# A two-layer hybrid block on one core: half-column inverse levels, and attention scores of both partition halves in turn

## Chip, cores, metric

The kernel runs on one core of one Trainium2 chip. The metric is the device time of one execution in microseconds (us). Everything below is float32 data; products of the large projections are done in two or three passes on a rounded part and a remainder (fp32r), the small ones inside the mixer in plain float32.

## What is computed

The reference is a stack of two layers over 256 positions of width 1024. Each layer is a half-weighted SwiGLU block, a mixer of three branches with gates, and a second SwiGLU block:

```python
for l in range(DEPTH):                                    # DEPTH = 2
    x = x + 0.5 * swiglu(rms_norm(x, ffa_norm[l]), ffa_w_in[l], ffa_w_out[l])
    h = rms_norm(x, mix_norm[l])
    (c_q, c_kv, k_rope, g_q, g_k, g_v, g_b, g_a, g_z, m_qkv, gate_logits) = split_cols(h @ w_in[l], IN_SPLITS)
    o_mla = mla_branch(...)                               # causal attention, 8 heads, 96 wide
    o_gdn = gdn_branch(...)                               # gated delta rule, 4 heads, 128 wide
    o_moba = moba_branch(...)                             # block attention, 8 heads, 64 wide
    up = jnp.einsum('bsnw,nwd->bsnd', branches, w_branch[l])
    x = x + jnp.sum(sigmoid(gates) * up, axis=2) @ w_out[l]
    x = x + 0.5 * swiglu(rms_norm(x, ffb_norm[l]), ffb_w_in[l], ffb_w_out[l])
```

With 256 positions the block attention has a single block, so it is causal attention with 64-wide heads. The delta rule needs the inverse of a unit lower triangular matrix for each half of 128 positions and each head; the reference solves with it, the kernel builds the inverse from 16x16 diagonal blocks and doubles the block size level by level.

## The kernel before

A phase (SwiGLU block or mixer) is a list of steps. A step loads one 512 KB tile of weights, splits it in two (a rounded part by ScalarE, line 260, a remainder by VectorE, line 261) and multiplies it on TensorE (lines 280 to 282, 309 and 311, 340 to 342, 965 and 966). `phase` walks the steps; between half steps it calls `tick`, which lets every spawned generator emit its next piece. A `yield n` in a generator waits for n ticks. So small work (attention, delta rule, epilogues) is laid between half steps of 12 large matmuls (lines 340 to 342; 8 for lines 965 and 966), and each engine runs what it was given in about the order in which it was emitted.

Names that matter here:

- `acc` and `pm` (lines 113 to 125) hand out PSUM banks from one pool of `BANKS` = 6; at most three are accumulators in the mixer, and `hold` lets at most `BANKS` - 4 = 2 score tiles be held at once. `done` gives the hold back once the exponentials that read the tile have been emitted.
- `attention` (line 560) serves the causal attention (heads 96 wide) and the block attention. Its `plan` has entries "s0" (scores of the first 128 queries, four heads, 128 keys each), "s1" (scores of the second 128 queries, two heads, 256 keys each) and "o" (two heads' product with the values); between entries it waits `Y_ATT` = 3 ticks. `scores` issues one matmul for each head (line 574), adds the mask with one bf16 matmul against an identity (line 576), takes the row maximum on VectorE (lines 581 and 582), one tick later the exponentials on ScalarE (line 586, each followed by a read of its accumulated sum), and a tick after that the reciprocal (line 590) and the scaling by it (line 592). `outputs` waits until the four tiles of its two heads exist, transposes the probabilities on TensorE (lines 604 to 606), copies them out of PSUM (line 608), and multiplies them with the values (lines 613 and 614): the first head writes partitions 0 to 63 of one bank, the second 64 to 127.
- In the block attention (plan at line 1078) even heads lie on partitions 0 to 63 of the transposed queries and keys, odd heads on 64 to 127. Each score tile holds heads of one half: "s0" with (0, 2, 4, 6), then (1, 3, 5, 7); "s1" with (0, 2), (1, 3), (4, 6), (5, 7).
- `invert` (line 731) is the inverse, for both halves c = 0, 1 of the positions. After `small` has brought the 16x16 blocks it runs two levels (loop at line 769): four matmuls, one for each head, of the coupling blocks with the inverse so far (line 772), a ScalarE copy (line 774), a GpSimd product for the next level (line 776), four matmuls with the transposed inverse (line 780), and a VectorE sum (line 783) that keeps only the even blocks' columns: of 128 columns, blocks of 16 (then 32) columns at even places, 64 in all. `back` (line 665) then transposes the result (line 669) and copies it (line 670). A third level on 64x64 quarters follows (lines 789 to 796).
- A float32 matmul shows as two weight loads and two matmul records in the trace. Records of four heads therefore count eight.

Of the kernel before, what the change touches and what calls it, by code (L numbers as in the profile page):

```python
# [11 lines left out]
AF = mybir.ActivationFunctionType  # L12
OP = mybir.AluOpType
AX = mybir.AxisListType
# [23 lines left out]
BANKS = 8 - NTP  # L38
# [43 lines left out]
class Kern:  # L82
# [32 lines left out]
        self.held["acc"] += 1  # L115
        return self.ps.tile([128, 512], F32, name=self.nm("acc"), tag="bank", bufs=BANKS)

    def hold(self):

        while self.held["pm"] >= BANKS - 4:  # L120
            yield 1
        self.held["pm"] += 1

    def done(self, what):
        self.held[what] -= 1
# [434 lines left out]
    def attention(self, plan, getq, getk, getv, rq, oT):  # L560
# [3 lines left out]
        nc = self.nc  # L564
# [1 line left out]
        P0, P1 = {}, {}  # L566
        left = [len(plan)]

        def scores(hs, n, w, q0, dst):
            t = q0 // 128  # L570
            yield from self.hold()
            ps = self.pm().rearrange("p (h k) -> p h k", h=n)
            for i, h in enumerate(hs):
                mm(ps[:, i, :], getq(h)[:, q0:q0 + 128], getk(h)[:, 0:w], start=(i == 0), stop=False,  # L574
                   skip_group_check=True)
            mm(ps[:, :, w - 128:w], self.identb, self.maskA[:, None, :].to_broadcast([128, n, 128]), start=False, stop=True,
               skip_group_check=True)
            dh = hs[1] - hs[0]
            rqs = rq[t][:, hs[0]:hs[-1] + 1:dh]
            mx, nb, sm, rs = (self.sm(4)[:, 0:n] for _ in range(4))  # L580
            nc.vector.tensor_reduce(mx, ps, axis=AX.X, op=OP.max)
            nc.vector.scalar_tensor_tensor(nb, mx, -1.0, rqs, op0=OP.mult, op1=OP.mult)
            yield 1
            P = self.b2().rearrange("p (h k) -> p h k", h=n)
            for h in range(n):
                nc.scalar.activation(P[:, h, :], ps[:, h, :], AF.Exp, scale=rqs[:, h:h + 1], bias=nb[:, h:h + 1],
                                     accum_out=sm[:, h:h + 1])
            self.done("pm")
            yield 1
            nc.vector.reciprocal(rs, sm)  # L590
            for h in range(n):
                nc.scalar.activation(P[:, h, :], P[:, h, :], AF.Copy, scale=rs[:, h:h + 1])
            for i, h in enumerate(hs):
                dst[h] = P[:, i, :]
            left[0] -= 1

        def outputs(hs):
            while not all(h in P0 and h in P1 for h in hs):
                yield 1
            yield 1  # L600
            PT = []
            for h in hs:
                pt = self.tp().rearrange("p (j k) -> p j k", j=4)
                nc.tensor.transpose(pt[:, 0, :], P0[h], self.ident)
                nc.tensor.transpose(pt[:, 1, :], P1[h][:, 0:128], self.ident)
                nc.tensor.transpose(pt[:, 2, :], P1[h][:, 128:256], self.ident)
                PT.append(self.b2())
                nc.scalar.copy(PT[-1][:, 0:384], pt[:, 0:3, :].rearrange("p j k -> p (j k)"))
            yield 1
            o = self.pm()[:, 0:256]  # L610
            for i, h in enumerate(hs):
                ov = o[64 * i:64 * i + 64, :]
                mm(ov, getv(0, h), PT[i][:, 0:256], start=True, stop=False, skip_group_check=True)  # L613
                mm(ov[:, 128:256], getv(1, h), PT[i][:, 256:384], start=False, stop=True, skip_group_check=True)
            k = hs[0] // 2
            self.split(oT[k // 2][:, k % 2, 0, :], oT[k // 2][:, k % 2, 1, :], o)
            left[0] -= 1

        for what, hs in plan:
            if what == "o":  # L620
                yield from outputs(hs)
            else:
                self.spawn(scores(hs, 4, 128, 0, P0) if what == "s0" else scores(hs, 2, 256, 128, P1))
            yield Y_ATT
# [3 lines left out]
    def gdn(self, ready, sil, beta, g, zs, oT):  # L628


        nc = self.nc
# [107 lines left out]
        def invert(c):  # L739
# [27 lines left out]
            back(zz[:, :, 0, :], zz[:, :, 1, :])  # L767
            yield 1
            for l in range(LEVELS - 1):
                p = v4(self.pm())  # L770
                for h in range(H):
                    mm(p[:, h, :], cm[:, h, :], zz[:, h, 0, :], start=True, stop=True)
                t1 = v4(self.b2())
                nc.scalar.copy(t1, p)
                cm = v4(self.b2())
                nc.gpsimd.tensor_tensor(cm, nk, brow(self.lev[l + 1]), op=OP.mult)
                yield Y_INV
                p = v4(self.pm())
                for h in range(H):
                    mm(p[:, h, :], zz[:, h, 1, :], t1[:, h, :], start=True, stop=True)  # L780
                even = lambda z: z.rearrange("p h (m s b) -> p h m s b", s=2, b=16 << l)[:, :, :, 0, :]
                v = even(zz[:, :, 0, :])
                nc.vector.tensor_tensor(v, even(p), v, op=OP.add)
                yield Y_INV
                back(zz[:, :, 0, :], zz[:, :, 1, :])

# [95 lines left out]
    def mixer(self, l, norm_after):  # L882
# [177 lines left out]
        def attend():  # L1060
# [11 lines left out]
            while not all(("turned", ("mT", i), 1) in d for i in range(2)) or ("mv", 1) not in d:  # L1072
# [2 lines left out]
            d["oT", 2] = [newT() for _ in range(2)]  # L1075
            sl = lambda z, h: z[64 * (h % 2):64 * (h % 2) + 64, h // 2, :]
            yield from self.attention(
                [("s0", (0, 2, 4, 6)), ("s0", (1, 3, 5, 7)), ("s1", (0, 2)), ("s1", (1, 3)), ("o", (0, 1)),
                 ("s1", (4, 6)), ("o", (2, 3)), ("s1", (5, 7)), ("o", (4, 5)), ("o", (6, 7))],
                lambda h: sl(d["mT", 0], h), lambda h: sl(d["mT", 1], h),  # L1080
                lambda tt, h: d["mv", tt][:, h, :], [d["mr", 0], d["mr", 1]], d["oT", 2])
            d["o", 2] = True
# [215 lines left out]
```

## Time and profile before

| | |
|---|---|
| time, median of 3 runs | 1350.1 us (1348.01 to 1353.65) |
| profiled execution | 1350.52 us, of which its span 1348.5 us |
| TensorE (PE) busy | 1320.3 us (98% of the span) |
| weight loads (PEld) busy | 1150.3 us (85%) |
| VectorE (DVE) busy | 937.4 us (70%) |
| ScalarE (ACT) busy | 786.9 us (58%) |
| GpSimd (POOL) busy | 117.9 us (9%) |
| granted TensorE clock | 1.0 over the whole span |

Busy time of PE counts from the start of a record to its modelled end, and records overlap in the pipeline; the distance from one start to the next tells what a matmul costs. The mixers lie at about 200 to 490 us and 866 to 1157 us. In each of them the inverse's levels and the block attention run together in the stretch of some 80 us that begins with the first block score tile (340 us and 1005 us).

### The profile page before, as it was taken

What the parts mean: (1) busy time and instruction counts of PE and PEld (TensorE: products, weight loads), DVE (VectorE), ACT (ScalarE), POOL (GpSimd) and SP (SyncE); (2) the same over time, 40 slices, a digit from 0 to 9 for tenths busy, and PEclk for the clock granted to TensorE, in tenths of its full rate; (3) what the DMA queues carried; (4) which work ended last, traced back from release to release, by engine and by line L of the source; (5) the groups of instructions that cost most, each with busy time, mean ns of one, the idle gap of its engine ahead of it and who ended that gap; (6) DMA issues with size and microseconds to landing.
All of it is one profiled execution on the core that took longest, in us unless ns stands there. A gap on an engine that the chain in (4) does not pass through costs nothing.

```text
span 1348.5 us, 21398 instructions
## 1 busy us (share of the span) xinstructions
PE 1320.3 (98%) x7786; PEld 1150.3 (85%) x7786; DVE 937.4 (70%) x1890; ACT 786.9 (58%) x1783; POOL 117.9 (9%) x157
## 2 busy tenths in 40 slices
PE   6999999999999999999999999999999999999998
PEld 5888888788999988888888888887889999888887
DVE  6777558888457677775577775588865576777752
ACT  6666447776654556664466654487656544666642
POOL 0010003711101000000000000044120000000000
PEclk9999999999999999999999999999999999999999
DMA  8765566566343657665666556555553445666551
GB/s 277 233 221 185 177 181 167 145 169 176 103 131 110 188 156 218 188 189 176 197 196 194 185 176 184 158 173 160 153 157 99 139 127 171 187 188 189 191 184 62
DMA packets 207561, 231.25 MB, mean 171 GB/s; under 512 B 15616, under 2 KB 166112, under 8 KB 207456
## 3 DMA queue, kind: packets, MB, share of 16 engines
q1 hardware_dynamic: 207456, 229.89, 56.4%
q8 instruction: 61, 1.00, 0.3%
q14 instruction: 44, 0.36, 0.1%
HBM read 227.11 MB, written 2.75 MB: 170 GB/s over the span
## 4 chain that ended last, share of the span: by engine, by line
PE 92%; DVE 3%; ACT 2%; POOL 1%; DMA 1%; issue 1%; SPq 0%; DVEq 0%; ACTq 0%; POOLq 0%
PE acc L309 22%; PE acc L311 11%; PE acc L280 10%; PE acc L282 10%; PE acc L281 10%; PE acc L340 5%; PE acc L341 5%; PE acc L342 5%; PE acc L965 3%; PE pm L574 2%; PE acc L966 1%; ACT wh L260 1%; DMA raw<-in_ffa_w_in 1%; DVE wl L261 1%; PE tp L370 1%; PE pm L613 1%
## 5 line engine op out<-in xcount | busy, mean ns | idle before, releaser
L261 DVE TENSOR_TENSOR wl<-raw,wh 128x512 fp32r<-128x512 f32 (+1 forms) x844 | 563.2, 687 | 265.7 <-ACT wh L260 265.4
L260 ACT CAST wh<-raw 128x512 fp32r<-128x512 f32 (+1 forms) x844 | 497.2, 619 | 389.7 <-issue 147.4
L309 PE MATMUL acc<-q,wh 128*128 128x512 f32 x1280 | 449.3, 396 | 0.0
L311 PE MATMUL acc<-q,wl 128*128 128x256 f32 x1280 | 359.2, 281 | 0.0
L309 PEld LDWEIGHTS acc<-q,wh 128*128 128x128 f32 x1280 | 240.1, 188 | 55.8
L280 PE MATMUL acc<-wh,q 128*128 128x512 f32 (+2 forms) x656 | 259.1, 395 | 1.4 <-ACT q L358 1.4
L282 PE MATMUL acc<-wh,q 128*128 128x512 f32 (+2 forms) x656 | 256.1, 390 | 0.0
L281 PE MATMUL acc<-wl,q 128*128 128x512 f32 (+2 forms) x656 | 255.5, 390 | 0.0
L311 PEld LDWEIGHTS acc<-q,wl 128*128 128x128 f32 x1280 | 242.4, 189 | 0.5
L340 PE MATMUL acc<-q,wh 128*128 128x256 f32 x576 | 168.3, 292 | 0.0
L341 PE MATMUL acc<-q,wh 128*128 128x256 f32 x576 | 163.2, 283 | 0.4 <-DVE q L359 0.4
L342 PE MATMUL acc<-q,wl 128*128 128x256 f32 x576 | 163.0, 283 | 0.0
L280 PEld LDWEIGHTS acc<-wh,q 128*128 128x128 f32 x656 | 123.9, 189 | 26.3 <-ACT q L358 2.4
L282 PEld LDWEIGHTS acc<-wh,q 128*128 128x128 f32 x656 | 123.5, 188 | 26.2 <-DVE q L359 2.2
L281 PEld LDWEIGHTS acc<-wl,q 128*128 128x128 f32 x656 | 123.8, 189 | 21.7
L340 PEld LDWEIGHTS acc<-q,wh 128*128 128x128 f32 x576 | 110.3, 192 | 1.8 <-issue 1.0
L341 PEld LDWEIGHTS acc<-q,wh 128*128 128x128 f32 x576 | 110.3, 191 | 1.2 <-DVE q L359 0.8
L342 PEld LDWEIGHTS acc<-q,wl 128*128 128x128 f32 x576 | 110.1, 191 | 0.1
L965 PE MATMUL acc<-q,wh 128*128 128x512 f32 x192 | 70.5, 406 | 0.0
L486 DVE TENSOR_TENSOR d<-d,acc 128x256 f32<-128x256 f32 x160 | 66.5, 416 | 5.3 <-ACT d L484 5.3
L484 ACT COPY d<-acc 128x256 f32<-128x256 f32 x160 | 58.8, 368 | 18.9 <-PE acc L311 18.8
L392 POOL TENSOR_TENSOR s<-s,mhalf 128x1 f32<-128x1 f32 x12 | 8.3, 691 | 634.3 <-DVE s L385 634.3
(203 smaller groups left out, 1280.9 us busy)
## 6 DMA issues: line engine op xcount, KB each, us to landing
raw<-in_w_in SPq DMA_DIRECT2D x104, 512.0 KB
raw<-in_ffa_w_in SPq DMA_DIRECT2D x88, 512.0 KB
raw<-in_ffb_w_in SPq DMA_DIRECT2D x88, 512.0 KB
raw<-in_ffa_w_out SPq DMA_DIRECT2D x44, 512.0 KB
raw<-in_ffb_w_out SPq DMA_DIRECT2D x44, 512.0 KB
raw<-in_w_branch SPq DMA_DIRECT2D x24, 512.0 KB
raw<-in_w_out SPq DMA_DIRECT2D x16, 512.0 KB
raw<-in_w_in SPq DMA_DIRECT2D x8, 416.0 KB
```

What stands on the lines that cost most here:

```text
L260: nc.scalar.copy(s.wh[:, v], s.raw[:, v])
L261: nc.vector.tensor_sub(s.wl[:, v], s.raw[:, v], s.wh[:, v].bitcast(F32))
L280: mm(o, xh, wh[:, j, :], start=(k == 0), stop=False)
L281: mm(o, xh, wl[:, j, :], start=False, stop=False)
L282: mm(o, xl, wh[:, j, :], start=False, stop=(k == nk - 1))
L309: mm(ps.rearrange("p (s c) -> p s c", s=2), wh[:, k, v], x2, start=(g == 0 and k == 0), stop=False, skip_group_check=True)
L311: mm(ps[:, 0:256], wl[:, k, v], x2[:, 0, :], start=False, stop=last, skip_group_check=True)
L340: mm(o, wh[:, k, v], xh, start=(g == 0 and c == 0 and k == 0), stop=False, skip_group_check=True)
L341: mm(o, wh[:, k, v], xl, start=False, stop=False, skip_group_check=True)
L342: mm(o, wl[:, k, v], xh, start=False, stop=(4 * g + k == nk - 1), skip_group_check=True)
L486: nc.vector.tensor_tensor(dst, dst, ps[:, 0:256], op=OP.add)
L965: mm(p, wh[:, k, :], self.X[k // 2][:, k % 2], start=(k == 0), stop=False, skip_group_check=True)
```

## The change

Three edits, all in the mixer:

1. In `invert`, the first two levels multiply only the even blocks' columns of the inverse, 64 of 128 for each head. The matmuls of lines 772 and 780, the ScalarE copy and the PSUM tiles are half as wide; the moving operand of line 772 is read with gaps, and VectorE's sum reads a packed tile.
2. In `attention`, a score entry can hold two groups. For the block attention, the groups of the even and the odd heads go into one entry: `hold(2)` for two banks at once, the matmuls of the two groups alternating head by head, then both masks, both maxima; a tick later all exponentials, another tick later all scalings. The plan has 7 entries instead of 10. The causal attention still has one group for each entry.
3. In `outputs`, the two heads' first products are issued one after the other, then the two second products.

```diff
-    def hold(self):
-
-        while self.held["pm"] >= BANKS - 4:
-            yield 1
-        self.held["pm"] += 1
+    def hold(self, n=1):
+
+        while self.held["pm"] + n > BANKS - 4:
+            yield 1
+        self.held["pm"] += n
...
-        def scores(hs, n, w, q0, dst):
+        def scores(groups, n, w, q0, dst):
+
             t = q0 // 128
-            yield from self.hold()
-            ps = self.pm().rearrange("p (h k) -> p h k", h=n)
-            for i, h in enumerate(hs):
-                mm(ps[:, i, :], getq(h)[:, q0:q0 + 128], getk(h)[:, 0:w], start=(i == 0), stop=False,
-                   skip_group_check=True)
-            mm(ps[:, :, w - 128:w], self.identb, self.maskA[:, None, :].to_broadcast([128, n, 128]), start=False, stop=True,
-               skip_group_check=True)
...
+            yield from self.hold(len(groups))
+            banks = [self.pm().rearrange("p (h k) -> p h k", h=n) for _ in groups]
+            for i in range(n):
+                for hs, ps in zip(groups, banks):
+                    mm(ps[:, i, :], getq(hs[i])[:, q0:q0 + 128], getk(hs[i])[:, 0:w], start=(i == 0), stop=False,
+                       skip_group_check=True)
+            for ps in banks:
+                mm(ps[:, :, w - 128:w], self.identb, self.maskA[:, None, :].to_broadcast([128, n, 128]), start=False,
+                   stop=True, skip_group_check=True)
+            made = []
+            for hs, ps in zip(groups, banks):
+                rqs = rq[t][:, hs[0]:hs[-1] + 1:hs[1] - hs[0]]
+                mx, nb = (self.sm(4)[:, 0:n] for _ in range(2))
+                nc.vector.tensor_reduce(mx, ps, axis=AX.X, op=OP.max)
+                nc.vector.scalar_tensor_tensor(nb, mx, -1.0, rqs, op0=OP.mult, op1=OP.mult)
+                made.append((hs, ps, rqs, nb))
+            yield 1
+            soft = []
+            for hs, ps, rqs, nb in made:
+                P, sm = self.b2().rearrange("p (h k) -> p h k", h=n), self.sm(4)[:, 0:n]
+                for h in range(n):
+                    nc.scalar.activation(P[:, h, :], ps[:, h, :], AF.Exp, scale=rqs[:, h:h + 1], bias=nb[:, h:h + 1],
+                                         accum_out=sm[:, h:h + 1])
+                self.done("pm")
+                soft.append((hs, P, sm))
+            yield 1
+            for hs, P, sm in soft:
...
-            for i, h in enumerate(hs):
-                ov = o[64 * i:64 * i + 64, :]
-                mm(ov, getv(0, h), PT[i][:, 0:256], start=True, stop=False, skip_group_check=True)
-                mm(ov[:, 128:256], getv(1, h), PT[i][:, 256:384], start=False, stop=True, skip_group_check=True)
+            halves = [(o[64 * i:64 * i + 64, :], h, PT[i]) for i, h in enumerate(hs)]
+            for ov, h, pt in halves:
+                mm(ov, getv(0, h), pt[:, 0:256], start=True, stop=False, skip_group_check=True)
+            for ov, h, pt in halves:
+                mm(ov[:, 128:256], getv(1, h), pt[:, 256:384], start=False, stop=True, skip_group_check=True)
...
             for l in range(LEVELS - 1):
-                p = v4(self.pm())
+                even = lambda z: z.rearrange("p h (m s b) -> p h m s b", s=2, b=16 << l)[:, :, :, 0, :]
+                half = lambda z: z[:, 0:256].rearrange("p (h c) -> p h c", h=H)
+                v = even(zz[:, :, 0, :])
+                p = half(self.pm())
                 for h in range(H):
-                    mm(p[:, h, :], cm[:, h, :], zz[:, h, 0, :], start=True, stop=True)
-                t1 = v4(self.b2())
+                    mm(p[:, h, :], cm[:, h, :], v[:, h], start=True, stop=True)
+                t1 = half(self.b2())
...
-                p = v4(self.pm())
+                p = half(self.pm())
                 for h in range(H):
                     mm(p[:, h, :], zz[:, h, 1, :], t1[:, h, :], start=True, stop=True)
-                even = lambda z: z.rearrange("p h (m s b) -> p h m s b", s=2, b=16 << l)[:, :, :, 0, :]
-                v = even(zz[:, :, 0, :])
-                nc.vector.tensor_tensor(v, even(p), v, op=OP.add)
+                nc.vector.tensor_tensor(v, p.rearrange("p h (m b) -> p h m b", b=16 << l), v, op=OP.add)
...
-                [("s0", (0, 2, 4, 6)), ("s0", (1, 3, 5, 7)), ("s1", (0, 2)), ("s1", (1, 3)), ("o", (0, 1)),
-                 ("s1", (4, 6)), ("o", (2, 3)), ("s1", (5, 7)), ("o", (4, 5)), ("o", (6, 7))],
+                [("s0", (0, 2, 4, 6), (1, 3, 5, 7)), ("s1", (0, 2), (1, 3)), ("o", (0, 1)), ("s1", (4, 6), (5, 7)),
+                 ("o", (2, 3)), ("o", (4, 5)), ("o", (6, 7))],
```

## Rows read from the trace of the kernel before

**Rows 1.** The page: its span, the busy time of the engines, and the chain of work that ended last by engine.

```profile
span 1348.5 us, 21398 instructions
...
PE 1320.3 (98%) x7786; PEld 1150.3 (85%) x7786; DVE 937.4 (70%) x1890; ACT 786.9 (58%) x1783; POOL 117.9 (9%) x157
...
PE 92%; DVE 3%; ACT 2%; POOL 1%; DMA 1%; issue 1%; SPq 0%; DVEq 0%; ACTq 0%; POOLq 0%
```

**Rows 2.** The view by windows, for the two stretches in which the inverse and the block attention run: us, then busy us (and instructions) of PE, PEld, DVE, ACT and POOL, then the granted clock, the DMA share and GB/s.

```profile
340.00:420.00 80.00, 80.00 (x636) 73.66 (x634) 45.61 (x91) 48.64 (x119) 2.81 (x4) 1.00 0.42 119
...
1005.00:1085.00 80.00, 80.00 (x635) 73.65 (x634) 45.22 (x91) 48.59 (x119) 1.30 (x1) 1.00 0.41 119
```

**Rows 3.** The view by line and shape, PE alone: count, busy us, mean ns of one record.

```profile
L574 PE MATMUL pm<-q,q 64*128 64x256 f32 x32 | 9.0, 402 | 0.0
...
L772 PE MATMUL pm<-q,d 128*128 128x128 f32 x64 | 8.5, 275 | 0.0
L780 PE MATMUL pm<-d,q 128*128 128x128 f32 x64 | 8.4, 275 | 0.0
...
L574 PE MATMUL pm<-q,q 64*128 64x128 f32 x32 | 4.6, 285 | 0.0
```

**Rows 4.** The timeline of the weight loads (PEld): one group of line 683, whose matmuls have a single moving column, and one of line 780, whose matmuls have 128.

```profile
318.66 0.19 PEld L342 LDWEIGHTS acc<-q,wl 128*128 128x128 f32 x1
318.78 1.88 PEld L683 LDWEIGHTS tp<-cst,q 128*128 128x128 f32 x16
...
343.06 0.98 PEld L780 LDWEIGHTS pm<-d,q 128*128 128x128 f32 x8
```

**Rows 5.** The timeline of PE around the second "s0" group of the block attention: start, us, then the record.

```profile
347.47 0.28 PE L340 MATMUL acc<-q,wh 128*128 128x256 f32 x1
...
347.70 0.28 PE L342 MATMUL acc<-q,wl 128*128 128x256 f32 x1
347.91 1.16 PE L574 MATMUL pm<-q,q 64*128 64x128 f32 x8
349.00 0.39 PE L576 MATMUL pm<-cb 128*128 128x512 bf16 x1
...
349.35 0.28 PE L341 MATMUL acc<-q,wh 128*128 128x256 f32 x1
```

**Rows 6.** The timeline of PE around the first "s1" group of the block attention.

```profile
356.06 0.28 PE L342 MATMUL acc<-q,wl 128*128 128x256 f32 x1
356.27 1.13 PE L574 MATMUL pm<-q,q 64*128 64x256 f32 x4
357.33 0.28 PE L576 MATMUL pm<-cb 128*128 128x256 bf16 x1
...
357.57 0.28 PE L341 MATMUL acc<-q,wh 128*128 128x256 f32 x1
```

**Rows 7.** The timeline of PE at two masks of the causal attention, where no change of shape stands ahead of them.

```profile
265.00 0.38 PE L576 MATMUL pm<-cb 128*128 128x512 bf16 x1
...
265.45 0.28 PE L966 MATMUL acc<-q,wl 128*128 128x256 f32 x1
...
270.28 0.28 PE L576 MATMUL pm<-cb 128*128 128x256 bf16 x1
...
270.62 0.40 PE L281 MATMUL acc<-wl,q 128*128 128x512 f32 x1
270.86 0.39 PE L282 MATMUL acc<-wh,q 128*128 128x512 f32 x1
```

**Rows 8.** The timeline of PE at one product with the values (two heads, each two matmuls of 256 and of 128 columns).

```profile
291.08 0.66 PE L613 MATMUL pm<-d,d 128*64 128x256 f32 x4
291.56 0.40 PE L614 MATMUL pm<-d,d 128*64 128x128 f32 x4
291.89 0.50 PE L965 MATMUL acc<-q,wh 128*128 128x512 f32 x1
```

**Rows 9.** The timeline of ACT over the first score groups of the block attention; in brackets its idle time ahead of the row and what ended it.

```profile
343.42 0.46 ACT L586 ACTIVATE d<-pm,s,s 128x128 f32<-128x128 f32 x1 [1.87 <-DVE s L582]
...
345.09 0.20 ACT L586 ACTIVATION_READ_ACCUMULATOR d<-pm,s,s 128x1 f32 x1
345.54 1.28 ACT L592 ACTIVATE d<-d,s 128x128 f32<-128x128 f32 x4 [0.25 <-DVE s L590]
...
350.74 1.14 ACT L260 CAST wh<-raw 128x512 fp32r<-128x512 f32 x2 [2.89 <-PE acc L341]
351.78 0.58 ACT L670 COPY q<-tp 128x512 f32<-128x512 f32 x1
352.26 0.59 ACT L774 COPY d<-pm 128x512 f32<-128x512 f32 x1
...
356.61 0.62 ACT L1121 ACTIVATE d<-acc 128x512 f32<-128x512 f32 x1
...
359.13 0.56 ACT L586 ACTIVATE d<-pm,s,s 128x256 f32<-128x256 f32 x1 [0.87 <-DVE s L582]
...
360.14 0.19 ACT L586 ACTIVATION_READ_ACCUMULATOR d<-pm,s,s 128x1 f32 x1
360.57 0.91 ACT L592 ACTIVATE d<-d,s 128x256 f32<-128x256 f32 x2 [0.23 <-DVE s L590]
```

**Rows 10.** The timeline of PE at the second product of the second level, c = 0, one tick after the first "s1" group.

```profile
358.89 1.06 PE L780 MATMUL pm<-d,q 128*128 128x128 f32 x8
```

More of the change, by code (lines that the diff above doesn't have):

```diff
@@ L567, in attention @@
         left = [len(plan)]
-        def scores(hs, n, w, q0, dst):
+        def scores(groups, n, w, q0, dst):
             t = q0 // 128
-            yield from self.hold()
-            ps = self.pm().rearrange("p (h k) -> p h k", h=n)
-            for i, h in enumerate(hs):
-                mm(ps[:, i, :], getq(h)[:, q0:q0 + 128], getk(h)[:, 0:w], start=(i == 0), stop=False,
-                   skip_group_check=True)
-            mm(ps[:, :, w - 128:w], self.identb, self.maskA[:, None, :].to_broadcast([128, n, 128]), start=False, stop=True,
-               skip_group_check=True)
[L578 to L582, printed above, removed]
-            yield 1
[L584 to L588, printed above, removed]
-            yield 1
-            nc.vector.reciprocal(rs, sm)
-            for h in range(n):
-                nc.scalar.activation(P[:, h, :], P[:, h, :], AF.Copy, scale=rs[:, h:h + 1])
-            for i, h in enumerate(hs):
-                dst[h] = P[:, i, :]
@@ L595, in scores @@
+            yield 1
+            for hs, P, sm in soft:
+                rs = self.sm(4)[:, 0:n]
+                nc.vector.reciprocal(rs, sm)
+                for h in range(n):
+                    nc.scalar.activation(P[:, h, :], P[:, h, :], AF.Copy, scale=rs[:, h:h + 1])
+                for i, h in enumerate(hs):
+                    dst[h] = P[:, i, :]
             left[0] -= 1
@@ L610, in outputs @@
             o = self.pm()[:, 0:256]
-            for i, h in enumerate(hs):
-                ov = o[64 * i:64 * i + 64, :]
-                mm(ov, getv(0, h), PT[i][:, 0:256], start=True, stop=False, skip_group_check=True)
-                mm(ov[:, 128:256], getv(1, h), PT[i][:, 256:384], start=False, stop=True, skip_group_check=True)
+            halves = [(o[64 * i:64 * i + 64, :], h, PT[i]) for i, h in enumerate(hs)]
[3 more added lines that the diff above has]
+                mm(ov[:, 128:256], getv(1, h), pt[:, 256:384], start=False, stop=True, skip_group_check=True)
             k = hs[0] // 2
@@ L617, in outputs @@
             left[0] -= 1
-        for what, hs in plan:
+        for what, *hs in plan:
             if what == "o":
-                yield from outputs(hs)
+                yield from outputs(hs[0])
             else:
```

## Prediction

> **What bounds the kernel.** I read the page first: TensorE is busy for 98% of the span and the chain that ended last is 92% TensorE [rows 1]. So the question of every edit is whether it shortens TensorE's own queue, or makes that queue wait. The view by windows says the same of the two stretches that hold the edits: PE is busy 80.00 of 80.00 us in both, at a granted clock of 1.00 (2.4 GHz), while ACT has 48.6 us and DVE 45 us of work and the DMA share is about 0.4 [rows 2]. A record's duration overlaps with its neighbours', so I never multiply durations; I take distances from one start to the next out of the timeline. All sums are made against the profiled execution, 1350.5 us (1348.5 span and 2.0 around it), which stands 0.4 us over the median of the three runs.
>
> **Edit 1, the inverse on half the columns.** Lines 772 and 780 have 64 records each [rows 3]: two layers, two halves c, two levels, four heads, two records for a matmul. Columns fall from 128 to 64. What does a record cost? The weight loads of line 780 (128 columns) take 0.98 us for eight; taking off the length of one, 0.19 (line 342's row), leaves 0.79 for seven distances, 0.113 us. Line 683 multiplies the same 128x128 weights with a single column: 1.88 - 0.19 over 15 distances is 0.113 us again [rows 4]. One column and 128 columns cost the same, so 64 in between cost the same: each record has its own weight load, and the load sets the pace. The saving on TensorE is 0. The other end of the bound is a cost by columns: half of 128 x 0.113 us, 7.2 us. I take 0, since the row with one column lies beyond the edit and shows no gain. Reading the moving operand with gaps has no row; even at half the rate, 64 columns would take no longer than 128 do now, which the load covers. The eight ScalarE copies of line 774 become shorter; ScalarE is not the bound, so that pays nothing, but it helps below.
>
> **Edit 2, scores of both halves in turn.** First today's price of a group. An "s0" group stands between line 342 at 347.70 and the second large matmul after it at 349.35, 1.65 us, where without it two distances would stand, 0.23 (as from 347.47 to 347.70): 1.42 us [rows 5]. An "s1" group: 357.57 - 356.06 - 0.23 = 1.28 us [rows 6]. The mask is part of it: 512 columns and a large matmul take 0.45 us from 265.00 to 265.45, a large one alone 0.24, so the mask takes 0.21; with 256 columns 0.34 - 0.24 = 0.10 [rows 7]. Eight score records at 0.113 are 0.90, so 1.42 - 0.90 - 0.21 = 0.31 of "s0" is the change of the array's shape, into 64 rows and back; for "s1", four records of 0.21 (256 columns, twice, at 2.4 GHz) give 1.28 - 0.85 - 0.10 = 0.33.
>
> If the two partition halves run side by side, a pair costs one group, a second mask, and about 0.02 for the later start of the second half (my allowance). "s0": 1.42 + 0.21 + 0.02 = 1.65 for 2.84, saved 1.19. "s1": 1.28 + 0.10 + 0.02 = 1.40 for 2.56, saved 1.16. A layer has one pair of the first and two of the second: 3.51; two layers: 7.0 us.
>
> Do they run side by side? Before, no two matmuls of different row halves stand next to each other, so no row shows it. The nearest is the product with the values: two heads on two column halves. Line by line their records would take 4 x 0.21 + 4 x 0.107 = 1.28 us one after the other; from 291.08 to the next large matmul at 291.89 are 0.81 us, a drain of about 0.2 included [rows 8]. So column halves do run side by side, both their loads and their columns, and in plain float32. I take that for row halves too; the other bounds are below, and the lowest of them is worse than nothing.
>
> The Trainium skill, TensorEngine Tiling (Array Packing), section Key Properties, says that tiles load and multiply independently and that only a change of the tiling shape drains the array; by it the pair saves what I sum up here. No row of this case shows that for row halves.
>
> **What edit 2 queues.** The maxima, exponentials and scalings of a pair come in one lump. Most exposed is the first "o" entry: its transposes need the scalings of heads 0 and 1, two ticks after these are emitted. ScalarE's list from 343.42 on, from today's rows [rows 9]: exponentials of "s0" twice 1.87 (343.42 to 345.29), scalings twice 1.28, two pairs of casts of 1.14, two copies of 0.58 and two of 0.59, exponentials of "s1" twice 1.20 (359.13 to 360.33), and three of its scalings at 0.45: 14.7 us, so done at 358.1; with line 1121 (0.62) and one more pair of casts ahead of them, at 359.9. TensorE gets there thus: line 780 today at 358.89 [rows 10], plus 0.23 for the "s0" pair, less 0.02 and the 1.28 of the group that is gone, plus its own 0.90: 358.7. So a wait of 0 to 1.2 us for each layer; I take 0.2, near the lower end, because the scalings are emitted ahead of that line 1121 and those casts. The later "o" entries have their tiles many ticks earlier. The casts for the large matmuls queue behind the lump by some 3 us; they have that time, since ScalarE sat idle for 2.89 us ahead of the casts at 350.74 until a matmul freed a buffer [rows 9]: they run as far ahead as the buffers let them. `hold(2)` waits at build time only, and nothing else holds tiles in this stretch. The attention ends some 10 ticks earlier, for which nobody waits.
>
> **Edit 3, products in turn.** They run side by side already [rows 8], so 0. The added order: the first head's second product now stands behind the second head's first, and so behind the wait for the second head's copy (line 608). If that copy is late the first head's second product is late too, but it then runs beside the second head's, which ends last either way.
>
> **Sum.** 7.0 - 2 x 0.2 = 6.6 us: 1350.5 - 6.6 = 1343.9 us.
>
> **Rivals.**
> - *In program order.* TensorE starts matmuls strictly in order, so the second half can only overlap the second record of a head with the first record of the next. A pair then ends one record later: 0.11 for "s0", 0.21 for each "s1", 1.1 us in all: saved 5.5, 1345.0 us. Against it: in [rows 8] all four records of line 613 come ahead of line 614's, though the code issues both lines of the first head before any of the second's. The Trainium skill, TensorE: Matmul & The Clock Gate, Part 3, states this rule (matmuls start and end in program order); by it the time is this rival's, and the row disagrees with it.
> - *Weight loads of row halves take turns.* Loads of 128 columns then bound "s0" (16 x 0.113): it saves only one shape change, 0.31; "s1", with 0.21 of columns for a load, still overlaps. 2 x (0.31 + 2.32) - 0.4 = 4.9: 1345.6 us.
> - *The change doesn't do what it says: no overlap of row halves at all.* Then only one shape change for each pair is saved, 0.31 + 2 x 0.33 for a layer, 1.9 us: 1348.6 us. For it: no row shows the overlap.
> - *Each turn from half to half costs like a shape change*, 0.15: 7 + 3 + 3 turns are 2.0 us for a layer against 0.97 saved: 1352.5 us. Against it: the turns in [rows 8] cost nothing visible.
> - *Slower: a bank is missing.* A pair takes two of six banks at once, and the second is free only when both groups' exponentials are done: for "s0" at 343.42 + 3.74 = 347.2. Line 780 comes at 343.4; if its bank is that one, TensorE stands 3.8 us. For "s1" the exponentials begin 2.9 us after the group does and end 2.4 later, while the next claim comes after about 2.8: 2.5 us. With all six pairs hit, 2 x (3.8 + 2.5 + 2.5) = 17.6: 1350.5 - 7.0 + 17.6 = 1361.1 us. It decides from 1.2 us for each pair. Against it: PE is never idle in these stretches today [rows 2], and four banks remain, of which the large matmuls use one or two at a time.
> - *Columns count after all in edit 1*: 7.2 us more, 1336.7. Against it [rows 4].
>
> **How the numbers follow.** The forecast has 0.62, program order 0.08, loads in turn 0.07, no overlap 0.09, costly turns 0.03, a missing bank 0.06, columns 0.03, and 0.02 is left for what I don't see. The forecast's own range, by the wait of 0 to 1.2 and the spread of runs, is 1342 to 1346.5. The range of 8 in 10 takes in the first four cases: 1341.0 to 1349.5. A difference of 0.5% is about what a measurement of this kernel can tell from no change; that is 6.75 us, 1343.35 from the median. The forecast lies a little on the near side of that bound; I give it 0.45 below. With the case of columns: faster 0.32. Slower needs more than 1356.9, which only the missing bank and the unseen reach: 0.07. Same: 0.61.
>
> **What would show it.** Distances of line 780's weight loads still 0.113 (else edit 1 is wrong). Score records of one pair in 0.9 us, not 1.8, with both halves interleaved, and one pair about 1.65 us ("s0") or 1.40 ("s1") between large matmuls. Line 613 as in [rows 8]. A wait of TensorE for ScalarE ahead of line 604 for heads 0 and 1, under 1.2 us. A wait of line 780, 772 or a large matmul at its first record after a pair, released by line 586, would mean the missing bank and make the forecast wrong.

## The result

The changed kernel takes 1342.77 us in the median of 13 runs (1339.42 to 1347.98), the kernel before 1352.36 us in 13 runs beside it (1348.01 to 1355.51). The ratio is 0.9941, with a 95% interval of [0.9927, 0.9954]: faster by 8.0 us, by 6.2 at the least and 9.9 at the most. (The ratio is not the quotient of the two medians; these stand 9.6 us apart.) The forecast was 1343.9 us, a gain of 6.6.

The profiled execution is the longest of the 13, 1347.98 us with a span of 1345.8 us, so it is read for places and distances, not for its end. Its page answers to [rows 1]:

```profile
span 1345.8 us, 21412 instructions
...
PE 1318.3 (98%) x7786; PEld 1147.9 (85%) x7786; DVE 937.9 (70%) x1890; ACT 785.2 (58%) x1783; POOL 118.3 (9%) x157
...
PE 92%; DVE 3%; DMA 1%; ACT 1%; POOL 1%; issue 1%; SPq 0%; DVEq 0%; ACTq 0%; POOLq 0%
```

TensorE is still the bound, with as many records. Line numbers of the changed kernel differ: scores are line 576 (574 before), masks 579, transposes of the probabilities 614 to 616, values 623 and 625, the levels' products 787 and 795 (772 and 780), `back`'s transposes 680 (669).

**The pairs.** The timeline of PE around the "s0" pair, which answers to [rows 5], and around the first "s1" pair, for [rows 6]:

```profile
340.73 0.28 PE L342 MATMUL acc<-q,wl 128*128 128x256 f32 x1
340.94 1.16 PE L576 MATMUL pm<-q,q 64*128 64x128 f32 x16
342.03 0.60 PE L579 MATMUL pm<-cb 128*128 128x512 bf16 x2
342.29 0.47 PE L340 MATMUL acc<-q,wh 128*128 128x256 f32 x1
342.60 0.28 PE L341 MATMUL acc<-q,wh 128*128 128x256 f32 x1
...
348.44 0.28 PE L342 MATMUL acc<-q,wl 128*128 128x256 f32 x1
348.64 1.13 PE L576 MATMUL pm<-q,q 64*128 64x256 f32 x8
349.71 0.39 PE L579 MATMUL pm<-cb 128*128 128x256 bf16 x2
349.86 0.36 PE L340 MATMUL acc<-q,wh 128*128 128x256 f32 x1
350.06 0.28 PE L341 MATMUL acc<-q,wh 128*128 128x256 f32 x1
```

Sixteen score records now take the 1.16 us that eight took, and eight take the 1.13 of four. From line 342 to the second large matmul after it are 1.87 and 1.62 us; less the two distances that would stand there anyway, 1.63 and 1.39, against 1.65 and 1.40 in the forecast. In the single records the first matmuls of the two halves start 7 ns apart (340.938 and 340.945 us), and each half keeps its pace of 0.111 us.

**The levels.** The weight loads of line 795 in the same stretch, which answer to [rows 4], and the view by line and shape for [rows 3]:

```profile
343.67 0.19 PEld L342 LDWEIGHTS acc<-q,wl 128*128 128x128 f32 x1
343.79 0.98 PEld L795 LDWEIGHTS pm<-d,q 128*128 128x128 f32 x8
```

```profile
L787 PE MATMUL pm<-q,d 128*128 128x64 f32 x64 | 8.8, 286 | 0.0
...
L795 PE MATMUL pm<-d,q 128*128 128x64 f32 x64 | 8.0, 268 | 0.0
```

Eight loads take 0.98 us with 64 moving columns, as they did with 128: the load sets the pace, and edit 1 saves no time on TensorE.

**The end of the exponentials' lump.** The timeline of PE at the first "o" entry, where I had put 0.2 us of waiting per layer:

```profile
358.22 0.28 PE L342 MATMUL acc<-q,wl 128*128 128x256 f32 x1
358.34 1.00 PE L795 MATMUL pm<-d,q 128*128 128x64 f32 x8
359.18 0.28 PE L614 MATMUL tp<-ident,d 128*128 128x128 f32 x1
```

There is none: the transposes follow the level's products without a gap.

**A wait that the forecast did not see.** The view of PE's waits (us in total, how often, the longest), before and then after:

```profile
PE tp L669 <- DMA q<-zd: 4.5, 4, 1.4
...
PE pm L821 <- ACT d L837: 1.4, 2, 0.7
PE acc L280 <- ACT q L358: 1.4, 1, 1.4
PE tp L476 <- ACT d L471: 0.4, 1, 0.4
```

```profile
PE tp L680 <- DMA q<-zd: 5.0, 4, 1.5
...
PE acc L280 <- ACT q L358: 1.4, 1, 1.4
PE tp L476 <- ACT d L471: 1.0, 1, 1.0
```

Before, TensorE stood twice for 0.70 us ahead of the delta rule's product of line 821, which needs ScalarE's copy of the state, line 837. After, that wait is gone. (The waits ahead of line 476, 0.4 to 1.1 us, and of line 669 or 680, 4.2 to 5.6 us in all, differ from trace to trace in kernels of either kind, experiments 8 and 9 aside; no gain or loss is read from them.) The timeline of PE of the kernel before shows why it was there, and ScalarE's list beside it:

```profile
421.45 1.06 PE L835 MATMUL pm<-d,d 128*128 128x128 f32 x8
423.21 1.16 PE L821 MATMUL pm<-d,q 128*128 128x128 f32 x8 [0.70 <-ACT d L837]
```

```profile
421.53 1.14 ACT L260 CAST wh<-raw 128x512 fp32r<-128x512 f32 x2 [4.14 <-PE acc L341]
422.58 0.58 ACT L837 COPY d<-pm 128x512 f32<-128x512 f32 x1
```

The state's product (835) and its consumer (821) stood next to each other, and the copy between them lay behind two casts. In the changed kernel six large matmuls stand between product and consumer. My reading is that the plan has fewer entries, so that the later pieces fall into other ticks; experiments 1 to 3 show that it is edit 2 that takes the wait away.

So per layer the pairs save 3.48 us by distances (two "s0" groups of 1.405 against 1.63; four "s1" groups of 1.27 against two pairs of 1.39) and the vanished wait 0.70, 4.18 together: 8.4 us for two layers, beside 8.0 measured.

The length of a mixer shows it more sharply than the time of a run: from line 370's transposes ahead of it to those behind it. The timeline of PE at the two ends of the first mixer, before and then after:

```profile
201.47 0.65 PE L370 MATMUL tp<-ident,d 128*128 128x128 f32 x4 [0.47 <-DVE d L396]
...
493.63 0.66 PE L370 MATMUL tp<-ident,d 128*128 128x128 f32 x4 [0.53 <-DVE d L396]
```

```profile
201.97 0.66 PE L370 MATMUL tp<-ident,d 128*128 128x128 f32 x4 [0.47 <-DVE d L396]
...
490.10 0.65 PE L370 MATMUL tp<-ident,d 128*128 128x128 f32 x4 [0.53 <-DVE d L396]
```

These are 292.16 us before and 288.13 after: 4.0 us for one mixer, 8.0 for two. The sum of 4.18 is 0.2 too large, and the traces do not say where. The second mixer takes 292.07 us before and 290.78 in this execution, which lost 2.7 us there because the clock fell (experiments 4 and 8 to 11); in the trace of experiment 4, where it did not fall in the second mixer, it takes 288.08.

Much of what makes executions differ lies outside the edit. In the traces of all the kernels, whichever edits they have, each of the three SwiGLU blocks behind the first mixer takes one of two lengths, about 2.1 us apart: 185.9 or 188.0 us, 185.2 or 187.4, and 185.9 or 188.0. Why is not shown.

### The profile page after: what moved, and what is told of

Its sections match the earlier page's. It is cut to its first block, busy times and chain, and to the rows that moved or that the text cites. A ratio compares the mean times of both kernels' runs of the same rounds, so it can differ in the third digit from the quotient of the medians.

```text
span 1345.8 us, 21412 instructions
## 1 busy us (share of the span) xinstructions
PE 1318.3 (98%) x7786; PEld 1147.9 (85%) x7786; DVE 937.9 (70%) x1890; ACT 785.2 (58%) x1783; POOL 118.3 (9%) x157
## 4 chain that ended last, share of the span: by engine, by line
PE 92%; DVE 3%; DMA 1%; ACT 1%; POOL 1%; issue 1%; SPq 0%; DVEq 0%; ACTq 0%; POOLq 0%
PE acc L309 22%; PE acc L311 11%; PE acc L280 10%; PE acc L282 10%; PE acc L281 10%; PE acc L340 5%; PE acc L341 5%; PE acc L342 5%; PE acc L978 3%; PE acc L979 1%; PE pm L576 1%; DMA raw<-in_ffa_w_in 1%; ACT wh L260 1%; PE tp L370 1%; PE pm L623 1%; DVE wl L261 1%
```

## Experiments

Ratios are to the kernel before, run on the same chip in the same turn.

**1. Edit 1 alone.** The kernel before, with the levels on the even blocks' columns:

```diff
-                    mm(p[:, h, :], cm[:, h, :], zz[:, h, 0, :], start=True, stop=True)
+                    mm(p[:, h, :], cm[:, h, :], v[:, h], start=True, stop=True)
```

> The kernel before with edit 1 alone (the two levels on 64 of 128 columns). Theory: each record's pace is its 128-column weight load, about 0.112 us with 1, 64 or 128 moving columns, so a group of four heads still stands for about 1.13 us between large matmuls, and the time is that of before: ratio 1.000, between 0.998 and 1.002. Rival (columns count): up to 7.2 us less, ratio 0.9947.

Measured: 1353.1 us, ratio 1.0006 [0.9994, 1.0018]. A gain of 7.2 us would be 0.9947. The rival is out; the loads of its line 784 still take the time of eight loads:

```profile
343.23 0.98 PEld L784 LDWEIGHTS pm<-d,q 128*128 128x128 f32 x8
```

**2. Edit 2 alone.** The kernel before, with the pairs of scores and the plan of 7 entries (the diff of `scores` and of the plan ahead of the prediction).

> The kernel before with edit 2 alone (score groups of both partition halves in one entry). Theory: all of the gain is here: 7.0 us from the six pairs, and 1.4 us because the product with the state S1 is now placed six large matmuls later, so TensorE no longer waits 0.7 us in each layer for ScalarE's copy of S1: 8.4 us, ratio 0.9938. Rival (the S1 wait is moved elsewhere, only the pairs pay): 7.0 us, 0.9948. Rival (edits 1 or 3 carry a part): clearly above 0.995.

Measured: 1345.64 us, ratio 0.9953 [0.9936, 0.9970]. That carries the gain, which edits 1 and 3 alone don't, and in its trace the wait ahead of the delta rule's product is gone too. The interval holds both of the numbers expected, so this run alone does not say whether the wait's 1.4 us count; experiment 7 looks at the wait by itself.

**3. Edit 3 alone.**

```diff
-                mm(ov, getv(0, h), PT[i][:, 0:256], start=True, stop=False, skip_group_check=True)
-                mm(ov[:, 128:256], getv(1, h), PT[i][:, 256:384], start=False, stop=True, skip_group_check=True)
+            for ov, h, pt in halves:
+                mm(ov, getv(0, h), pt[:, 0:256], start=True, stop=False, skip_group_check=True)
+            for ov, h, pt in halves:
+                mm(ov[:, 128:256], getv(1, h), pt[:, 256:384], start=False, stop=True, skip_group_check=True)
```

> The kernel before with edit 3 alone (products with the values in turn). Theory: the two heads' products run side by side already, so nothing changes: ratio 1.000 (0.998 to 1.002), an entry stands for the same 1.24 us between large matmuls to 0.02. Rival (matmuls start in program order, so issuing them in turn brings overlap): each of 16 entries would shrink by 0.1 us or more, 1.6 us, ratio 0.9988 or less.

Measured: 1352.33 us, ratio 1.0002 [0.9991, 1.0013]: nothing; the rival's 0.9988 lies outside. The delta rule's wait for the copy of the state still adds up to 1.5 us in this trace, and to 1.4 in that of experiment 1; only edit 2 takes it away.

**4. The changed kernel again**, as it is.

> The changed kernel once more, for a second profile. Theory: 0.994 again, and the 2.75 us that its first profile lost between 995 and 1005 us (clock at half for 6.8 us) and the 2.1 us lost slowly between 1173 and 1280 us are of that execution and not of the kernel: a second profile lacks them, with a span near 1340. Rival: they are there again.

Measured: 1346.39 us, ratio 0.9949 [0.9933, 0.9965]. The second half of the theory failed, and the rival holds: the span is 1344.0, and both losses are there again. The clock is at 0.5 (1.2 of 2.4 GHz) for 6.8 us from 334.3 on, where the first profile had it from 997.3; both times it fell during the second of two waits ahead of line 680 (333.87 to 335.35 us, and 996.54 to 998.08). And the last SwiGLU block again takes 188.0 us, 2.1 more than in the trace of the kernel before; but so it does in those of experiments 1 and 3, so that loss does not come with edit 2.

**5. The pair group by group.** The changed kernel, with all heads of one half issued before those of the other:

```diff
-            for i in range(n):
-                for hs, ps in zip(groups, banks):
+            for hs, ps in zip(groups, banks):
+                for i in range(n):
```

> The changed kernel, but a pair issues all heads of the first group and then all of the second, instead of in turn. Theory: TensorE starts a row half's matmul as soon as that half is free, whatever stands between in program order, as it does for lines 613 and 614; a pair still stands for 1.63 us (first score entry) and 1.39 us (second) beyond two large matmuls, ratio to before 0.994. Rival (strict program order): the second group starts only behind the last record of the first, a pair costs about 0.8 us more, six pairs 5 us, ratio near 0.9975.

Measured: 1344.83 us, ratio 0.9949 [0.9930, 0.9967], which no difference from the changed kernel can be read from. The timeline of PE says more:

```profile
340.64 1.71 PE L576 MATMUL pm<-q,q 64*128 64x128 f32 x16
...
348.90 1.14 PE L576 MATMUL pm<-q,q 64*128 64x256 f32 x8
```

The "s1" pair is as short as in turn (1.14 against 1.13), although all four records of one half were issued ahead of the other's: in the single records the halves start 13 ns apart. In the "s0" pair the second half's first load starts at 341.194 us, together with the sixth of the eight records issued ahead of it, and the scores take 1.71 us against 1.16. So TensorE reaches past some waiting records to another tile, but not past any number: taking turns is worth nothing for "s1" and 0.55 us for "s0", 1.1 us in all, which the times are too coarse to show; the lengths of the mixers below show it.

The traces do not record the order in which the matmuls reached TensorE, and it is not exactly the code's (see lines 340 and 341 under 9 to 11). But the code's order does tell: the two heads' first products with the values start 14 ns apart where the code issues one head whole (line 613 before) and 7 ns in turn (line 623 after), as the halves of the scores start 13 and 7 ns apart. And here as there the other tile's first record starts between the two records of one matmul, which no strict order of whole matmuls gives. Strict program order is out.

**6. Pairs of one half.** The changed kernel, with "s1" pairs whose groups both lie on the same partitions:

```diff
-                [("s0", (0, 2, 4, 6), (1, 3, 5, 7)), ("s1", (0, 2), (1, 3)), ("o", (0, 1)), ("s1", (4, 6), (5, 7)),
+                [("s0", (0, 2, 4, 6), (1, 3, 5, 7)), ("s1", (0, 2), (4, 6)), ("s1", (1, 3), (5, 7)), ("o", (0, 1)),
```

> The changed kernel, but the pairs of the second score entry hold heads of one and the same partition half: (0, 2) with (4, 6), then (1, 3) with (5, 7). Theory: no overlap within such a pair; what is left of its gain is one change of the array's shape, 0.33 us, so a pair stands for 1.28 + 0.85 + 0.10 = 2.2 us instead of 1.39: 4 x 0.83 = 3.3 us more than the changed kernel, ratio to before about 0.9963. Rival (the gain of a pair comes from fewer shape changes and fewer stretches between large matmuls, not from the two halves): about 0.994 as the changed kernel.

Measured: 1348.17 us, ratio 0.9973 [0.9959, 0.9987]; the expected 0.9963 lies inside, the rival's 0.994 outside. (The edit also puts the first "o" entry behind the second pair.) Its timeline of PE at the first "s1" pair:

```profile
348.21 1.99 PE L576 MATMUL pm<-q,q 64*128 64x256 f32 x8
```

The same eight records take 1.99 us on one half and 1.13 on two. It is the two halves that pay, not that groups are joined.

**7. The delta rule's wait.** The kernel before, with the state declared known one tick later, so that large matmuls come between:

```diff
-                st["S1"] = v4(self.b2())
-                nc.scalar.copy(st["S1"], p)
+                S1 = v4(self.b2())
+                nc.scalar.copy(S1, p)
                 yield 1
+                st["S1"] = S1
```

> The kernel before, with the state S1 made known to the second half's solve one tick later, so that its product (line 821) is no longer issued right behind the copy of S1 (line 837) that it needs. Theory: the 0.70 us that TensorE waits there in each layer goes, 1.4 us in all, ratio 0.9990, and it is the part of the change's gain beyond the pairs. Rival (the wait only moves to the next matmul of the solve): ratio 1.000 and the same 0.7 us ahead of another line.

Measured: 1350.78 us, ratio 0.9992 [0.9982, 1.0002]. The two waits of 0.70 us are gone from the trace, and a new one of 0.17 us for each layer stands at a later place:

```profile
437.62 0.28 PE L342 MATMUL acc<-q,wl 128*128 128x256 f32 x1
438.08 0.66 PE L865 MATMUL tp<-ident,d 128*128 128x128 f32 x4 [0.17 <-DVE d L861]
```

That makes 1.1 us by the trace, the 0.9992 of the ratio; the interval just holds 1, so the trace carries this, not the time. The mixers agree: 291.63 and 291.55 us, 0.5 less each.

**8. A later inverse.** The changed kernel's waits ahead of line 680 are for a transfer. Here the transposes come two ticks later:

```diff
-            yield Y_DMA + c
+            yield Y_DMA + 2 + c
```

> The changed kernel, with the inverse's first transposes two ticks later, so that TensorE doesn't wait for the 16x16 blocks' transfer (waits of 1.4 and 0.85 us ahead of line 669 in each layer before). Theory: about 2.2 us less in each layer than the changed kernel, 4.5 us, ratio to before near 0.9905; the solve, which needs the inverse, comes some 40 us later and isn't held up. Rival (the wait is for weights and shows up at the next large matmul): ratio 0.994 as the changed kernel.

Measured: 1348.79 us, ratio 0.9977 [0.9966, 0.9989]: slower than the changed kernel, against my theory. The wait moved, and grew:

```profile
331.47 0.41 PE L680 MATMUL tp<-ident,q 128*128 128x128 f32 x2 [0.78 <-DMA q<-zd]
...
332.40 0.56 PE L787 MATMUL pm<-q,d 128*128 128x64 f32 x4
335.40 0.39 PE L341 MATMUL acc<-q,wh 128*128 128x256 f32 x1 [2.44 <-DVE q L359]
335.63 0.28 PE L342 MATMUL acc<-q,wl 128*128 128x256 f32 x1
...
335.98 0.41 PE L342 MATMUL acc<-q,wl 128*128 128x256 f32 x1
336.19 0.41 PE L340 MATMUL acc<-q,wh 128*128 128x256 f32 x1
```

The large matmuls that were to fill it wait themselves, for VectorE's split of their operand (line 359). In the first profile of the changed kernel the waits here are 1.47 and 0.91 us, 2.4 together; now 0.78 and 2.44, 3.2. The last rows show the second loss: records start 0.21 us apart instead of 0.12, at a granted clock of 0.5. All 12 runs of this kernel have a mean clock of 0.997 or less.

**9 to 11. The clock.** The records of single runs give a mean clock for each. It is 0.998 or less in 22 of 54 runs of the kernels with edit 1 and the waits as they were (the changed kernel three times, experiments 1, 5 and 6), in 12 of 12 of experiment 8, and in 2 of 98 runs of those without edit 1 (the kernel before, experiments 2, 3, 7 and 10). (The expectation below says 20 of 49; a recount gives 21.) A mean of 0.998 is a coarse sign: one fall of 3.4 us gives 0.9987, printed as 0.999, and isn't counted. With 0.999 counted as well, to which the last microsecond of an execution can add (the clock is at 0.5 there too, with TensorE's work done), it is 40 of 54, 12 of 12 and 16 of 98: the same contrast. Three kernels were run together. In experiment 9, the changed kernel, eight useless transposes stand ahead of the four real ones in each of the two places:

```diff
-        def back(r, dst):
+        def back(r, dst, fill=0, src=None):
             p = v4(self.tp())
+            for i in range(fill):
+                nc.tensor.transpose(p[:, i % 4, :], src, self.ident)
...
-            back(zz[:, :, 0, :], zz[:, :, 1, :])
+            back(zz[:, :, 0, :], zz[:, :, 1, :], 8, st["z0", 0][:, 3, 0, :] if c else self.ident)
```

> The changed kernel with useless work in place of two waits: ahead of the transposes of the 16x16 blocks (line 680 of the changed kernel, where TensorE waited 1.47 and 0.91 us, then 1.07 and 1.54 us, for a transfer) stand eight more 128-column transposes each, 0.9 us by 0.113, into the same bank, overwritten afterwards; those ahead of the second wait read the first half's block. Nothing else is changed. So far the records of single runs show a mean clock of 0.998 or less in 20 of 49 runs of the kernels with edit 1 and in 2 of 81 of those without it; in the two traces of the changed kernel the clock falls to 0.5 for 6.8 us right behind these waits. Theory: it falls because TensorE stood still there, so with the waits filled nearly all runs show 0.999 or 1.0, and the median comes out 1 to 3 us under the changed kernel's on the same chip (1342 to 1345). Rival (the fall has another cause, the waits are a coincidence): the clock falls in 2 of 5 runs as before and the median stays or rises by up to 1 us, what the filling adds where a wait is shorter than it.

Experiment 10 is the changed kernel with the loop over the levels as it was before:

> The changed kernel without edit 1: the levels multiply all 128 columns again; pairs of scores and values in turn stay. Theory 1 (edit 1 saves nothing on TensorE, but makes the fall of the clock behind the waits ahead of line 680 more likely): nearly all runs at a clock of 0.999 or 1.0, and a median equal to the changed kernel's or up to 2 us below it. Rival (edit 1 harmless, the falls belong to the chips that the kernels ran on): the share of runs with a fallen clock is that of the changed kernel beside it, and the medians differ by less than 1 us. Rival (edit 1 pays something after all, by ScalarE's and VectorE's shorter work): the median is 2 us or more above the changed kernel's.

Experiment 11 is the changed kernel as it is:

> The changed kernel as it is, beside the two others on the same chip: ratio 0.994 to 0.996 to the kernel before, and a clock of 0.998 or less in a third to a half of its runs, as in its earlier ones (5 of 19).

| kernel | median us | ratio | runs with a clock of 0.998 or less | 0.999 or less |
|---|---|---|---|---|
| 9, waits filled | 1342.64 | 0.9923 [0.9905, 0.9942] | 0 of 4 | 0 of 4 |
| 10, without edit 1 | 1343.91 | 0.9929 [0.9911, 0.9948] | 0 of 6 | 0 of 6 |
| 11, changed kernel | 1345.71 | 0.9943 [0.9925, 0.9962] | 1 of 5 | 5 of 5 |

The 1 of 5 is less than the third to a half that I expected. The trace of experiment 11 has the fall in both layers. Its timeline of PE, and the view by windows (columns as in [rows 2]):

```profile
332.50 0.63 PE L680 MATMUL tp<-ident,q 128*128 128x128 f32 x4 [1.29 <-DMA q<-zd]
332.97 1.00 PE L787 MATMUL pm<-q,d 128*128 128x64 f32 x8
333.78 0.37 PE L340 MATMUL acc<-q,wh 128*128 128x256 f32 x1
333.98 0.28 PE L341 MATMUL acc<-q,wh 128*128 128x256 f32 x1
335.34 1.09 PE L680 MATMUL tp<-ident,q 128*128 128x128 f32 x4 [1.08 <-DMA q<-zd]
```

```profile
330.00:334.70 4.70, 2.98 (x20) 2.22 (x18) 3.83 (x5) 3.15 (x8) 1.99 (x2) 1.00 0.87 269
334.70:338.10 3.40, 2.76 (x13) 2.79 (x14) 2.22 (x4) 0.59 (x1) 3.40 (x3) 0.50 0.76 250
```

TensorE stood for 1.29 us, worked for 1.8, and stood again for 1.08; 0.4 us into this second wait the clock fell to 0.5, and the four transposes behind it took 1.09 us instead of 0.63. With the waits filled, the same stretch keeps 1.00:

```profile
330.00:334.00 4.00, 3.71 (x31) 3.29 (x30) 3.12 (x5) 3.03 (x7) 1.68 (x2) 1.00 0.95 291
334.00:338.00 4.00, 3.35 (x30) 3.15 (x29) 2.54 (x4) 0.59 (x1) 4.00 (x3) 1.00 0.69 233
```

What follows: that the fall goes with edit 1 is shown by the counts; that it needs the waits is made likely, by none in 4 with them filled (in that trace 0.28 and 0.65 us of waiting are left in the first mixer) and 12 of 12 with a wait of 2.44 us. All six falls in the traces of the changed kernel and of experiments 4, 5, 6 and 11 begin 0.3 to 0.8 us into the second wait. The Trainium skill, TensorE: Matmul & The Clock Gate, Part 1, says that the engine drops to its lower clock when it has been idle; the trace agrees as to the place. Waits alone do not decide it: the first mixer of the first profile has 1.47 and 0.91 us of them and keeps its clock. What it is in edit 1 stays open. It need not be the columns: with it, lines 340 and 341 come ahead of the second wait (333.78 and 333.98 above), while without it line 680 follows the levels' products at once, and the second wait takes 0.66 to 1.92 us with it and 0.86 to 1.43 without.

**The mixers alone.** What the medians blur, the lengths of the mixers in the traces show, read as in the result:

| kernel | first mixer, us | second mixer, us | clock at 0.5 for |
|---|---|---|---|
| before | 292.16 | 292.07 | |
| 1, edit 1 alone | 292.54 | 292.10 | |
| 2, edit 2 alone | 288.35 | 288.11 | |
| 3, edit 3 alone | 292.10 | 292.09 | |
| changed kernel | 288.13 | 290.78 | 6.8 us in the second |
| 4, changed kernel | 290.61 | 288.08 | 6.8 us in the first |
| 11, changed kernel | 288.89 | 288.79 | 3.4 us in each |
| 5, not in turn | 289.64 | 288.61 | 3.4 us in the first |
| 6, pairs of one half | 289.70 | 292.65 | 6.8 us in the second |
| 7, state later | 291.63 | 291.55 | |
| 8, later inverse | 290.05 | 290.02 | 3.4 us in each |
| 9, waits filled | 288.09 | 288.14 | |
| 10, without edit 1 | 288.24 | 288.18 | |

Edit 2 is the whole gain; edits 1 and 3 give nothing. Taking turns is worth 0.5 us for a mixer (experiment 5), the two halves 1.6 (experiment 6, where 1.7 was expected). A fall of the clock for 3.4 us costs 0.7 to 1.0 us, one for 6.8 us 2.5 to 3.0; in the first profile 6.0 us of work lie in the fallen stretch, at a pace of 0.21 us for 0.12, which makes 2.6 us. Filling the waits saves the falls and nothing else: without a fall the changed kernel's mixer is as short. In the medians of the three kernels the fall shows as 1.8 to 3.1 us, but their intervals overlap, and the runs of experiment 1 with a clock of 0.998 or less and those above it have the same mean (1353.3); that the kernel with the waits filled, the best of the study by its median, beats the changed kernel is not settled by the times.

## Why the prediction was right, step by step

**Edit 1 at nothing: right on TensorE.** The pace of a record is its weight load, as [rows 4] had it (experiment 1: 1.0006). The step lacked a side effect: with edit 1 the clock falls in the second wait ahead of line 680, in 22 of 54 runs by the stricter count and 40 by the looser.

**Edit 2, 3.51 us per layer: right in its mechanism and its size.** 3.48 by distances. The row halves overlap with loads and columns, as the column halves do in [rows 8]. The rivals on this step fall by the same rows: loads that take turns, a shape change at each turn and no overlap at all by the 16 records in 1.16 us, and program order by the halves' starts, 7 ns apart where a pair would have ended 0.11 us later, and by experiment 5. The Trainium skill, TensorE: Matmul & The Clock Gate, Part 3, has matmuls start and end in program order; that does not hold here: halves issued one behind the other start 13 ns apart.

**The wait for ScalarE's lump, 0.2 us per layer, 0.4 in all: mis-sized.** It measured 0. The upper end of 1.2 us assumed line 1121 and a pair of casts ahead of the scalings; the choice near the lower end was the better one.

**A missing bank: did not happen.** PE is busy for all of the stretch, as in [rows 2] (and for 80.00 of the 80 us from 1000 on):

```profile
340.00:420.00 80.00, 80.00 (x662) 74.85 (x661) 47.46 (x94) 49.12 (x121) 2.98 (x4) 1.00 0.44 126
```

**Edit 3 at nothing: right** (1.0002).

**What the sum lacked.** 1.4 us: the wait of line 821 for line 837, which stood in the trace of before at 423.2 and 1088.5 us. I had read the stretch from 340 to 420, where the edit lies, and not what a shorter plan does to the pieces behind it: with three entries fewer, later pieces move to other ticks. With it the sum is 2 x (3.48 + 0.70) = 8.4 where 6.6 was forecast and 8.0 measured.

**Where luck helped.** The forecast of 1343.9 us lies 1.1 us from the median of 1342.77, closer than its parts. It was counted from 1350.5 us; the kernel before took 1352.36 beside the changed one, and the gain was larger than forecast, so two misses partly cancel. By its own mark of 0.5% the result (0.59%, with an interval that reaches back over the mark) lies on the side to which it gave 0.32, not on the one with 0.61. Single executions of the changed kernel differ by up to 8.6 us, to which the SwiGLU blocks' two lengths and the falls of the clock both add.

## What to carry to other kernels

Where the contraction of small float32 products fits half the partitions, lay the operands on both halves and issue the halves in turn: here a second group then cost little more than its mask (0.22 us with a mask of 0.21, 0.12 with one of 0.10). Halving the moving columns of a product that is already bound by its weight load, here from 128 to 64, bought nothing. When an edit touches one stage, compare the length of that stage from trace to trace: here, where no clock fell, it repeats to 0.4 us, and whole executions of one kernel differ by 8.6. When a plan gets shorter, look through the whole chain behind it for pairs of producer and consumer that now stand closer together or further apart, and fill or move waits only where what comes next is ready: an idle stretch that moves can grow, and can take the clock with it.

## What the chip showed that was not expected

- The two row halves run both weight loads and matmuls side by side in plain float32: starts 7 ns apart in turn, 13 ns when one half's four records were issued first.
- Across tiles a matmul can start ahead of one issued before it, but the reach is limited: with eight records of one half ahead, the other half began with the sixth, 0.55 us late.
- During the second of two waits of 0.7 to 1.9 us each, with 1.8 us of work between them, the granted clock fell to 0.5 for 3.4 or 6.8 us in some executions and not in others of the same kernel. In the trace of experiment 8 it fell 0.6 and 0.9 us after a wait of 2.44 us had ended, and all 12 of its runs show a lowered clock.
- Three SwiGLU blocks that no edit touched each took one of two lengths, 2.1 us apart, from one execution to the next.
